# Experts in program order, one hint ahead of each branch, and token gathers by pairs of experts

## The chip, the cores and the metric

The kernel runs on one core of a Trainium2 chip. The metric is the time of one execution on the device in microseconds (us). It is written with a scheduler: the program text lists instructions in an order, the scheduler puts them into the order in which each engine's queue gets them, and it adds the semaphores. Only inside a block under `tc.manual_schedule()` do the engines get them in the order of the text.

## The reference

Two transformer blocks on 256 tokens of 1024 features, all in float32. The first (two layers) and the mixing half of the second are not touched here. The second block ends in a mixture of experts, which is what this case is about. A router gives each token its 4 best of 32 experts and their gates:

```
logits = xt @ w_router + b_router
top_val, top_idx = top_k(logits, 4);  gates = softmax(top_val)
```

For the tokens of an expert `e` it computes

```
gu = x_b @ w_gu[e] + b_gu[e]                      # 1024 -> 2048, gate and up interleaved
gate, up = min(gu[::2], 7), clip(gu[1::2], -7, 7)
((up + 1) * (gate * sigmoid(1.702 * gate))) @ w_dn[e] + b_dn[e]
```

and adds the result, times the gate, to the rows of its tokens. How many tokens an expert has is only known when the router has run. With these inputs, of the experts 1 to 31, 22 have at most 32 tokens, six (4, 13, 21, 24, 26, 30) have 33 to 64, and three (5, 14, 29) have 65 to 96; the profile shows it by which bodies run.

## The kernel before

**Weights.** An expert's weights are 12 tiles of 128 x 2048 float32 (1 MB): eight for gate and up (`ew.first(e)`), four for down (`ew.second(e)`). They pass through 18 buffers. `ew.load(n)` issues loads on SP up to tile `n`; tile `i` takes the buffer of tile `i - 18`, so SP waits until PE has read that one for the last time. The first 18 expert tiles are loaded before the experts start.

**Groups.** Tokens are worked on in groups of 32 (`GROUP`). A group's tokens are gathered by matmuls of the normed tokens `hf` with a one-hot matrix (`gather`, L1763; 32 matmuls in the trace, copied out by ACT and DVE into `xg`). `gather4` (L1773) does it for the first groups of four experts at once, 128 columns, in each fourth expert. `biased` (two matmuls) starts a group's sum in PSUM, `up` (64 matmuls in the trace, L1792) adds the product with the first eight tiles, `swiglu` makes the activation on DVE and ACT, `turn` transposes it (PE, then a copy on ACT into `hT`), `down` (64 matmuls, L1842) multiplies by the last four tiles, `parts` (ACT, DVE) scales by the gate and splits the result in two, and `scatter` (16 matmuls, L1856) adds it to the tokens' rows. The scatter matrix `sT` and the gates `gs` come from `slots_pick` (one-hots on DVE) and `slots` (PE, DVE, ACT).

**Branches.** Each engine reads the expert's count into a register (`values_load`, L1946) and tests it. After the first group's up comes `tc.If(n > 32)` (L1927), whose body gathers the tokens of groups 1 and 2 (`tokens`, 64 columns), runs up, slots, swiglu and turn for group 1, and in an inner `If(n > 64)` for group 2. After the first group's down comes a second `If` (L1942) with down, parts and scatter of those groups, again with an inner one (L1944). An `If` is one unit: nothing moves into it or out of it. At its end each engine sets its semaphore to what the body would have counted, so a buffer that the body could still read comes free for SP only when PE has passed the `If`. `tc.mark_branch_hint_location` writes, on PE, ACT and DVE, a hint that names where the coming branch will go (`label`), from the register `n`.

**Order.** Outside of the `If`s the scheduler chooses. In the trace the loads of the counts and the hints, which depend on nothing but the counts, stand far ahead of their place in the text, and the scatter of the expert before is woven into up. Expert 0 always has two groups, has no branch, and frees its first tiles one by one. A last `If` (L1955, label `more`) holds experts with over 96 tokens; it is not entered here.

The lines that matter below: L1792 up, L1842 down, L1856 scatter, L1825 and L1827 slots, L1809 turn, L1770 gather, L1339 the loads of weights on SP, L1927/L1930 and L1942/L1944 the branches, L1946 the counts, L2187 where the trace books the hints.

Of the kernel before, what the change touches and what calls it, by code (L numbers as in the profile page):

```python
# [74 lines left out]
def program(ctx: ExitStack, tc: tile.TileContext, a, out, dbg=None, upto=99, only=None):  # L75
# [1675 lines left out]
    def experts(hf, pool, ew, rest):  # L1751
        with ExitStack() as p3:
# [20 lines left out]
            def gather4(q):  # L1773

                oh = [same(t, q) for t in range(2)]
                xg = pool.tile([P, 8, P], F32, name="xg4", tag="xg4", bufs=1)
                c = slice(0 if q else GROUP, P)
                gather(xg[:, :, c], [o[:, c] for o in oh])
                return xg

# [6 lines left out]
            def up(ps, xg, W):  # L1787

                for k in range(8):
                    w = W(k)  # L1790
                    for b in range(4):
                        T.matmul(ps[32 * b:32 * b + 32], xg[:, k], w[:, 512 * b:512 * b + 512],  # L1792
                                 start=False, stop=k == 7, skip_group_check=True, tile_position=(0, 32 * b))

            def swiglu(pl, ps):
                gg = pl.tile([P, 256], F32, name="gg", tag="gg", bufs=2)
                V.tensor_scalar(gg, ps[:, :256], 7.0, None, op0=ALU.min)  # L1797
                tu = pl.tile([P, 2, 256], F32, name="etu", tag="etu", bufs=1)
# [5 lines left out]
                return gg  # L1804
# [61 lines left out]
            h0 = [pool.tile([P, 2, P], F32, name=f"hT{g}") for g in range(3)]  # L1866
            sT = [pool.tile([P, 2, 2, P], F32R, name=f"sT{g}") for g in range(4)]
            gs = [pool.tile([P, 1], F32, name=f"gs{g}") for g in range(4)]
# [3 lines left out]
            ohx = [pool.tile([P, 4, GROUP], F32, name=f"ohx{t}") for t in range(2)]  # L1872

            ps = [biased(eg(), 0) for g in range(2)]
            for k in range(8):
                for g in range(2):
                    for b in range(4):
                        T.matmul(ps[g][32 * b:32 * b + 32], ew.xg[:, k, GROUP * g:GROUP * g + GROUP], ew.first(0)(k)[:, 512 * b:512 * b + 512],
                                 start=False, stop=k == 7, skip_group_check=True, tile_position=(0, 32 * b))
                ew.load(NWE + k + 1)  # L1880
                if k == 3:
                    rest()
            hs = [swiglu(pool, p_) for p_ in ps]
            xg = gather4(0)
            ew.bias_of(1)
            for g in range(2):
# [304 lines left out]
```

## Time and profile before

| | |
|---|---|
| Time, median of 3 runs | 2630.83 us (2627.53 to 2643.96) |
| Profiled execution | 2639.72 us |
| Its span, first to last instruction | 2637.7 us |
| Mean granted clock of TensorE | 0.902 |
| Busy share of PE, PEld, DVE, ACT, POOL | 85, 61, 47, 29, 8% |
| DMA over the span | 244 GB/s, 644.16 MB |

PE is TensorE's matmuls, PEld its weight loads, whose queue (PEldq) also holds PE's register, branch and hint instructions. DVE is VectorE, ACT ScalarE, POOL GpSimd and SP SyncE, which only issues transfers. In rows of the timeline the columns are the start in us, the duration, engine, line, operation, output and inputs with their shapes, the count of merged instructions, and in brackets how long the engine had stood idle before and what released it. A busy PE is not a PE at its peak, and shares over the whole span mix stages with different limits: the two blocks ahead of the experts take until about 1505 us.

### The profile page before, as it was taken

The page shows a single profiled execution, that of the slowest core. Times are in us where ns is not written, and L with a number is a line of the kernel's source. Part 1 is how long each engine was busy: PE and PEld are TensorE (multiplying, and loading weights), DVE is VectorE, ACT ScalarE, POOL GpSimd, SP SyncE. Part 2 cuts the span into 40 slices and gives each one's busy share as a digit, 9 for nine tenths or more (in the row PEclk, how much of TensorE's full clock was granted, in tenths as well). Part 3 has the DMA queues.
Part 4 walks back from the last instruction along what each step waited for, and adds up shares of the span by engine and source line. Part 5 has one row for each costly group of instructions (what it writes and reads, how often), then busy time and mean ns, then how long its engine had stood idle before and what let it go on. Part 6 is the DMA issues. An engine that isn't in the chain of part 4 may idle for free. (4 is left out here: it accounts for less than half of the span.)

```text
span 2637.7 us, 43545 instructions
## 1 busy us (share of the span) xinstructions
PE 2230.7 (85%) x18012; PEld 1612.4 (61%) x18012; DVE 1240.6 (47%) x2385; ACT 753.3 (29%) x1336; POOL 203.2 (8%) x188
## 2 busy tenths in 40 slices
PE   8999789999997899988799975876778767787686
PEld 7898678988996679977667532433334324343343
DVE  4667977976657865579865411111111111111111
ACT  3554454444443544465333100000001000000001
POOL 0002310000003300025300000000000000000000
PEclk9999899999999999999889986888778877888897
DMA  8655234444485265442303778689997999888963
GB/s 314 216 194 195 108 133 155 163 145 160 152 322 181 97 266 193 156 135 82 110 17 128 290 318 364 258 328 413 416 378 295 377 417 417 361 339 356 416 284 114
DMA packets 97055, 644.16 MB, mean 244 GB/s; under 512 B 11776, under 2 KB 13312, under 8 KB 23296
## 3 DMA queue, kind: packets, MB, share of 16 engines
q1 hardware_dynamic: 91152, 628.33, 61.0%
q10 hardware_dynamic: 5616, 11.75, 1.4%
q8 instruction: 211, 3.46, 0.5%
q14 instruction: 76, 0.62, 0.1%
HBM read 638.98 MB, written 1.05 MB: 243 GB/s over the span
## 5 line engine op out<-in xcount | busy, mean ns | idle before, releaser
L684 DVE TENSOR_TENSOR wl<-wst,wh 128x1024 fp32r<-128x1024 f32 x298 | 363.7, 1224 | 229.2 <-ACT wh L682 222.6
L749 PE MATMUL gu<-xh,wl 128*128 128x256 f32 x1632 | 459.7, 282 | 7.9 <-DVE wl L684 5.2
L747 PE MATMUL gu<-xh,wh 128*128 128x256 f32 x1632 | 461.5, 283 | 2.1 <-ACT xh L730 1.4
L748 PE MATMUL gu<-xl,wh 128*128 128x256 f32 x1632 | 459.6, 282 | 0.0
L682 ACT CAST wh<-wst 128x1024 fp32r<-128x1024 f32 x320 | 333.5, 1050 | 349.6 <-PE gu L748 203.7
L747 PEld LDWEIGHTS gu<-xh,wh 128*128 128x128 f32 x1632 | 312.8, 192 | 13.4 <-ACT xh L730 3.7
L749 PEld LDWEIGHTS gu<-xh,wl 128*128 128x128 f32 x1632 | 312.7, 192 | 12.3 <-DVE wl L684 6.6
L748 PEld LDWEIGHTS gu<-xl,wh 128*128 128x128 f32 x1632 | 312.7, 192 | 3.2 <-issue 0.3
L1797 DVE TENSOR_SCALAR gg<-eg 128x256 f32<-128x256 f32 x45 | 19.1, 424 | 544.1 <-PE eg L1792 533.1
L1792 PE MATMUL eg<-ew,xg 128*32 128x512 f32 x1984 | 262.4, 672 | 0.0
L1842 PE MATMUL eg<-ew,hT 128*32 128x256 f32 x2880 | 201.9, 446 | 16.9 <-ACT hT L1810 15.5
L1800 ACT ACTIVATE etu<-gg 128x256 f32<-128x256 f32 x45 | 18.7, 416 | 631.3 <-DVE gg L1797 629.2
L1842 PEld LDWEIGHTS eg<-ew,hT 128*32 128x32 f32 x2880 | 101.4, 128 | 111.0 <-issue 40.5
L1792 PEld LDWEIGHTS eg<-ew,xg 128*32 128x32 f32 x1984 | 62.4, 122 | 159.6 <-issue 133.6
L1856 PE MATMUL ac<-y,sT 64*128 64x256 f32 x512 | 54.4, 304 | 102.0 <-PEq L1942 96.9
L104 PE MATMUL acc<-wh,hl 128*128 128x512 f32 x352 | 138.9, 395 | 0.6 <-DVE hl L731 0.6
L103 PE MATMUL acc<-wl,hh 128*128 128x512 f32 x352 | 138.2, 393 | 0.0
L102 PE MATMUL acc<-wh,hh 128*128 128x512 f32 x352 | 138.1, 393 | 0.0
L1856 PEld LDWEIGHTS ac<-y,sT 64*128 64x128 f32 x512 | 39.5, 187 | 146.0 <-issue 144.6
L1433 PE MATMUL pj<-hxH,wl 128*128 128x256 f32 x296 | 88.4, 299 | 14.6 <-DVE wl L1154 13.2
L1825 PE MATMUL ms<-ident,ohs 128*128 128x128 f32 x64 | 17.6, 370 | 98.1 <-PEq L1927 91.3
L1792 PE MATMUL eg<-ew,xgx 128*32 128x512 f32 x768 | 99.0, 674 | 0.0
(560 smaller groups left out, 3586.4 us busy)
## 6 DMA issues: line engine op xcount, KB each, us to landing
ew<-in_wexp SPq DMA_DIRECT2D x384, 1024.0 KB, 15.6
wst<-in_wgu SPq DMA_DIRECT2D x88, 1024.0 KB, 4.8
wst<-in_wd SPq DMA_DIRECT2D x44, 1024.0 KB, 4.8
wada<-in_wada SPq DMA_DIRECT2D x24, 1024.0 KB, 8.7
wst<-in_win SPq DMA_DIRECT2D x20, 1024.0 KB, 4.8
ws<-in_win SPq DMA_DIRECT2D x36, 512.0 KB, 3.8
wst<-in_wout SPq DMA_DIRECT2D x8, 1024.0 KB, 4.8
ws<-in_wup SPq DMA_DIRECT2D x8, 512.0 KB, 4.7
```

The lines of the kernel that those rows point to most:

```text
L102: T.matmul(o, lh, rh, start=start, stop=False)
L103: T.matmul(o, lh, rl, start=False, stop=False)
L104: T.matmul(o, ll, rh, start=False, stop=stop)
L682: S.copy(hi, s_)
L684: (G if kind == SHARED and h else V).tensor_tensor(lo, s_, hi.bitcast(F32), op=ALU.subtract)
L747: T.matmul(o, h[:, c0:c0 + P], st.xh[:, ts, k], start=k == 0, stop=False)
L748: T.matmul(o, h[:, c0:c0 + P], st.xl[:, ts, k], start=False, stop=False)
L749: T.matmul(o, l[:, c0:c0 + P], st.xh[:, ts, k], start=False, stop=k == 7)
L1433: T.matmul(ps[:, j], l[:, c0:c0 + P], hh[:, kk], start=False, stop=kk == 7, skip_group_check=True)
L1792: T.matmul(ps[32 * b:32 * b + 32], xg[:, k], w[:, 512 * b:512 * b + 512], start=False, stop=k == 7, skip_group_check=True, tile_position=( ...
L1842: T.matmul(ps[32 * c:32 * c + 32], hT[:, k % 2, 32 * (k // 2):32 * (k // 2) + 32], w[:, 256 * c:256 * c + 256], start=k == 0, stop=k == 7, ...
L1856: T.matmul(acc[t][h][:, 256 * v:256 * v + 256], sT[hs, v, t], x[hs], start=False, stop=False, skip_group_check=True)
```

## The change

All experts, 0 to 31, are now issued under `tc.manual_schedule()`, on all engines, in the order of the text: one load of the count and one hint ahead of each branch, scatter of the expert before behind the first `If`. Tokens are gathered for a pair of experts, two groups (64 columns) each, in every odd expert, so the second group needs no gather of its own. In the first `If` the second group has only up and swiglu; its slots and turn move into the second `If` (`rest_of`). A third group is gathered alone (32 columns). `gg`, `hT`, `sT` and `gs` have one buffer for the first group and one for further groups (three for `gg`).

```diff
             def same(t, q):
-                o = pool.tile([P, 4, GROUP], F32, name="oh4", tag="oh4", bufs=2)
-                V.tensor_tensor(o, bc(iota[:, :GROUP], 4, 1), bc(pos[t][:, 4 * q:4 * q + 4], GROUP, 2), op=ALU.is_equal)
+                o = pool.tile([P, 2, 2 * GROUP], F32, name=f"oh2{t}", tag=f"oh2{t}", bufs=1)
+                V.tensor_tensor(o, bc(iota, 2, 1), bc(pos[t][:, 2 * q:2 * q + 2], 2 * GROUP, 2), op=ALU.is_equal)
...
-            def gather4(q):
...
-            def up(ps, xg, W):
+            def up_row(ps, x, w, k):
+                for b in range(4):
+                    T.matmul(ps[32 * b:32 * b + 32], x, w[:, 512 * b:512 * b + 512],
+                             start=False, stop=k == 7, skip_group_check=True, tile_position=(0, 32 * b))
+
+            def up(e, xg, W):
+                ps = biased(eg(), e)
                 for k in range(8):
...
+                    up_row(ps, xg[:, k], W(k), k)
+                return ps
...
+            with tc.manual_schedule():
+                ps = [biased(eg(), 0) for g in range(2)]
+                for k in range(8):
                     for g in range(2):
+                        up_row(ps[g], ew.xg[:, k, GROUP * g:GROUP * g + GROUP], ew.first(0)(k), k)
+                    ew.load(NWE + k + 1)
+                    if k == 3:
+                        rest()
+                oh2 = [same(t, 0)[:, 2 * GROUP:] for t in range(2)]
                 for g in range(2):
+                    swiglu(gg[g], ps[g])
+                gather(xg[:, :, 2 * GROUP:], oh2)
+                ew.bias_of(1)
+                slots_pick(oh, 0, 0)
+                slots_pick(ohx, 0, 1)
+                turn(hT, gg[0])
+                turn(hTx, gg[1])
+                slots(sT, gs, oh, 0)
+                parts(y, down(hT, ew.second(0)), gs)
+                slots(sTx, gsx, ohx, 0)
+                parts(yx, down(hTx, ew.second(0)), gsx)
+                ew.load(12 + NWE)
+                slots_pick(oh, 1, 0)
+                scatter(sTx, yx)
...
             def tokens(e, g):
                 for t in range(2):
-                    V.tensor_scalar(ohg[t], iota, float(GROUP * g), pos[t][:, e:e + 1], op0=ALU.add, op1=ALU.is_equal)
+                    V.tensor_scalar(ohg[t], iota[:, :GROUP], float(GROUP * g), pos[t][:, e:e + 1], op0=ALU.add, op1=ALU.is_equal)
                 gather(xgx, ohg)
-            def group_up(e, g, i, W):
-                ps = biased(eg(), e)
-                up(ps, xgx[:, :, GROUP * i:GROUP * i + GROUP], W)
+            def rest_of(e, g, i, W):
                 slots_pick(ohx, e, g)
-                slots(sT[2 + i], gs[2 + i], ohx, e)
-                turn(h0[1 + i], swiglu(mpool, ps))
-            def group_down(i, W):
-                parts(yx, down(h0[1 + i], W), gs[2 + i])
-                scatter(sT[2 + i], yx)
...
+                turn(hTx, gg[i])
+                slots(sTx, gsx, ohx, e)
+                parts(yx, down(hTx, W), gsx)
+                scatter(sTx, yx)
...
+            with tc.manual_schedule():
+                n = count(1)
+                for e in range(1, NE):
+                    W1, W2 = ew.first(e), ew.second(e)
+                    x0 = 2 * GROUP * (e % 2)
+                    if e % 2 and e + 1 < NE:
+                        oh2 = [same(t, (e + 1) // 2) for t in range(2)]
+                    p_ = up(e, xg[:, :, x0:x0 + GROUP], W1)
+                    swiglu(gg[0], p_)
+                    with tc.If(n > GROUP, label=f"u{e}"):
+                        p_ = up(e, xg[:, :, x0 + GROUP:x0 + 2 * GROUP], W1)
+                        swiglu(gg[1], p_)
+                        with tc.If(n > 2 * GROUP):
+                            tokens(e, 2)
+                            swiglu(gg[2], up(e, xgx, W1))
+                    tc.mark_branch_hint_location(f"d{e}", hint=(n > GROUP), engines=engines)
+                    ew.load(12 * e + 8 + NWE)
+                    scatter(sT, y)
+                    slots(sT, gs, oh, e)
+                    if e % 2 and e + 1 < NE:
+                        gather(xg, oh2)
+                    turn(hT, gg[0])
+                    if e + 1 < NE:
+                        ew.bias_of(e + 1)
+                        slots_pick(oh, e + 1, 0)
+                    parts(y, down(hT, W2), gs)
+                    with tc.If(n > GROUP, label=f"d{e}"):
+                        rest_of(e, 1, 1, W2)
+                        with tc.If(n > 2 * GROUP):
+                            rest_of(e, 2, 2, W2)
+                    n = count(e + 1)
+                    if e + 1 < NE:
+                        tc.mark_branch_hint_location(f"u{e + 1}", hint=(n > GROUP), engines=engines)
+                    else:
+                        tc.mark_branch_hint_location("more", hint=(n > GROUPS * GROUP), engines=engines)
+                    ew.load(12 * e + 12 + NWE)
+                scatter(sT, y)
```

`count(e)` is the load of the count, as before (`values_load`).

## Rows read from the trace of the kernel before

**Rows 1.** Windows by stage: us, PE, PEld, DVE, ACT, POOL, PEclk, DMA share, GB/s.

```profile
1505.00:1512.00 7.00, 7.00 (x28) 2.01 (x31) 4.86 (x14) 0.00 (x0) 0.00 (x0) 0.55 0.01 2
...
1512.00:1650.00 138.00, 94.81 (x851) 45.37 (x847) 18.58 (x60) 9.43 (x22) 0.00 (x0) 0.80 0.84 340
...
1650.00:1760.00 110.00, 94.20 (x889) 47.32 (x885) 20.13 (x64) 10.14 (x25) 0.00 (x0) 0.88 0.67 268
...
1760.00:1970.00 210.00, 147.29 (x1181) 70.38 (x1185) 27.17 (x83) 12.69 (x30) 0.00 (x0) 0.80 1.01 416
...
1970.00:2070.00 100.00, 85.55 (x843) 43.86 (x839) 18.60 (x59) 10.28 (x24) 0.00 (x0) 0.90 0.72 287
...
2240.00:2520.00 280.00, 215.06 (x1862) 106.05 (x1861) 41.31 (x128) 20.78 (x49) 0.00 (x0) 0.83 0.91 371
...
2520.00:2610.00 90.00, 78.70 (x795) 36.91 (x798) 14.49 (x45) 8.43 (x20) 0.00 (x0) 0.91 0.54 214
```

**Rows 2.** DMA issues of the page: the expert weights.

```profile
ew<-in_wexp SPq DMA_DIRECT2D x384, 1024.0 KB, 15.6
```

**Rows 3.** Source view, register and branch instructions: count, ns min/median/max, first to last start.

```profile
L1946 PEldq TENSOR_LOAD <-cnt x31: 294/300/321, 1533.4 to 1596.5; - x31
...
L2187 PEldq BRANCH_PREFETCH_HINT  x62: 28/30/44, 1531.6 to 1597.0; - x62
...
L1927 PEldq COMPARE_BRANCH  x31: 73/5942/6882, 1555.0 to 2608.6; - x31
...
L1942 PEldq COMPARE_BRANCH  x31: 77/6112/6407, 1565.9 to 2619.6; - x31
...
L1944 PEldq COMPARE_BRANCH  x18: 76/216/1254, 1685.6 to 2601.3; - x18
```

**Rows 4.** Waits of PE and SP over the experts: us in total, times, longest.

```profile
PE ac L1856 <- PEq L1942: 96.9, 20, 5.1
...
PE ms L1825 <- PEq L1927: 91.3, 20, 17.6
...
SPq L1339 <- PEq L1927: 226.8, 21, 21.9
```

**Rows 5.** Timeline of PE, expert 10: one group.

```profile
1859.26 0.35 PE L1856 MATMUL ac<-y,sT 64*128 64x256 f32 x1 [4.89 <-PEq L1942]
...
1873.88 0.66 PE L1825 MATMUL ms<-ident,ohs 128*128 128x128 f32 x2 [3.76 <-PEq L1927]
...
1876.23 5.49 PE L1842 MATMUL eg<-ew,hT 128*32 128x256 f32 x64 [0.52 <-ACT hT L1810]
...
1886.72 0.47 PE L1856 MATMUL ac<-y,sT 64*128 64x256 f32 x1 [5.00 <-PEq L1942]
```

**Rows 6.** Timeline of PE, parts of experts 5, 7 and 30.

```profile
1716.94 0.44 PE L1809 MATMUL ms<-ident,gg 128*128 128x128 f32 x2 [1.70 <-DVE gg L1803]
...
1717.78 7.08 PE L1792 MATMUL eg<-ew,xgx 128*32 128x512 f32 x64
...
1740.16 3.66 PE L1842 MATMUL eg<-ew,hT 128*32 128x256 f32 x64
...
1744.47 1.49 PE L1856 MATMUL ac<-yx,sT 64*128 64x256 f32 x16 [0.64 <-ACT yx L1847]
...
1785.98 6.32 PE L1770 MATMUL ms<-oh,hf 128*128 128x128 f32 x32
...
2571.01 5.41 PE L1770 MATMUL ms<-ohg,hf 128*128 128x64 f32 x32 [1.71 <-DVE ohg L1905]
```

**Rows 7.** Timeline of PE, experts 29 to 31.

```profile
2500.91 0.35 PE L1856 MATMUL ac<-y,sT 64*128 64x256 f32 x1 [4.91 <-PEq L1942]
...
2559.64 0.28 PE L1856 MATMUL ac<-y,sT 64*128 64x256 f32 x1
...
2601.93 0.38 PE L1856 MATMUL ac<-y,sT 64*128 64x256 f32 x1 [0.82 <-PEq L1944]
...
2615.31 6.28 PE L1842 MATMUL eg<-ew,hT 128*32 128x256 f32 x64 [0.52 <-ACT hT L1810]
```

More of the change, by code (lines that the diff above doesn't have):

```diff
@@ L1872, in experts @@
             ohx = [pool.tile([P, 4, GROUP], F32, name=f"ohx{t}") for t in range(2)]
-            ps = [biased(eg(), 0) for g in range(2)]
-            for k in range(8):
-                for g in range(2):
[L1877 to L1886, printed above, removed]
-                slots_pick((oh, ohx)[g], 0, g)
-                slots(sT[3 * g], gs[3 * g], (oh, ohx)[g], 0)
-            for g in range(2):
-                turn(h0[g], hs[g])
-            for g in range(2):
-                parts((y, yx)[g], down(h0[g], ew.second(0)), gs[3 * g])
-            ew.load(12 + NWE)
+            xg = pool.tile([P, 8, P], F32, name="xg2")
+            with tc.manual_schedule():
+                ps = [biased(eg(), 0) for g in range(2)]
+                for k in range(8):
+                    for g in range(2):
+                        up_row(ps[g], ew.xg[:, k, GROUP * g:GROUP * g + GROUP], ew.first(0)(k), k)
[3 more added lines that the diff above has]
+                oh2 = [same(t, 0)[:, 2 * GROUP:] for t in range(2)]
+                for g in range(2):
+                    swiglu(gg[g], ps[g])
[12 more added lines that the diff above has]
+                scatter(sTx, yx)
             px.close()
@@ L1911, in group_up @@
                 slots_pick(ohx, e, g)
-                slots(sT[2 + i], gs[2 + i], ohx, e)
-                turn(h0[1 + i], swiglu(mpool, ps))
-            def group_down(i, W):
-                parts(yx, down(h0[1 + i], W), gs[2 + i])
-                scatter(sT[2 + i], yx)
-            scatter(sT[3], yx)
-            n = nc.values_load(ew.cnt[0:1, 1:2], min_val=0, max_val=256)
-            for e in range(1, NE):
-                W1, W2 = ew.first(e), ew.second(e)
-                p_ = biased(eg(), e)
-                slots_pick(oh, e, 0)
-                up(p_, xg[:, :, GROUP * (e % 4):GROUP * (e % 4) + GROUP], W1)
-                h = swiglu(pool, p_)
-                with tc.If(n > GROUP, label=f"u{e}"):
-                    tokens(e, 1)
-                    group_up(e, 1, 0, W1)
-                    with tc.If(n > 2 * GROUP):
-                        group_up(e, 2, 1, W1)
-                tc.mark_branch_hint_location(f"d{e}", hint=(n > GROUP), engines=engines)
-                ew.load(12 * e + 8 + NWE)
-                scatter(sT[(e - 1) % 2], y)
-                slots(sT[e % 2], gs[e % 2], oh, e)
-                if e % 4 == 3 and e + 1 < NE:
-                    xg = gather4((e + 1) // 4)
-                turn(h0[0], h)
-                if e + 1 < NE:
-                    ew.bias_of(e + 1)
-                parts(y, down(h0[0], W2), gs[e % 2])
-                with tc.If(n > GROUP, label=f"d{e}"):
-                    group_down(0, W2)
-                    with tc.If(n > 2 * GROUP):
-                        group_down(1, W2)
-                n = nc.values_load(ew.cnt[0:1, e + 1:e + 2], min_val=0, max_val=256)
-                if e + 1 < NE:
-                    tc.mark_branch_hint_location(f"u{e + 1}", hint=(n > GROUP), engines=engines)
-                else:
-                    tc.mark_branch_hint_location("more", hint=(n > GROUPS * GROUP), engines=engines)
-                ew.load(12 * e + 12 + NWE)
```

37 lines of the change are left out of this document (14 added, 23 removed).

## The prediction

> **What bounds the kernel now.** I read the page first (where the time lies), then the windows by stage, the source view of the branches and hints, PE's waits, and last the timeline of single experts. The experts run from about 1505 us to 2622 us of a span of 2637.7 us, so the change can only move these 1117 us.
>
> The DMA engines move 384 weight tiles of 1 MB [rows 2]. In a saturated stretch they run at 1.01 of their time and 416 GB/s (from 1760 us on, [rows 1]), so a tile of 1.049 MB takes 2.52 us and an expert of 12 tiles 30.2 us. Eighteen tiles are there before expert 0 starts; the queue stands at 2 GB/s until 1512 us [rows 1]. The other 366 tiles need 922 us. Against 416 GB/s the other windows lose 138 x (1 - 340/416) = 25 us, 110 x (1 - 268/416) = 39 us, 31 us, 30 us and, at the end, 44 us: 169 us of standing DMA. 1512 + 922 + 169 = 2603, which is where the last weights land. So the stage is limited by DMA except where buffers come free late, and PE frees them.
>
> What PE does in an expert with one group: 27.5 us from 1859.26 to 1886.72 [rows 5]. In it PE stands twice, 3.76 us at the branch of L1927 and 5.00 us at that of L1942. Over the stage this is 91 us and 97 us [rows 4], and SP waits 227 us for PE's sequencer at the first of them before it may issue loads [rows 4]. The cause is in the source view [rows 3]: the branch itself takes 5.9 and 6.1 us on PE (median of 31 each, minimum 0.07, when the body is entered). All 62 prefetch hints of PE stand between 1531.6 and 1597.0 us, while the branches run from 1555 to 2619: the hints and the loads of the counts were moved to the front in a bunch, far from their branches. There they also block PE's queue: one wait at the branch of L1927 is 17.6 us long [rows 4].
>
> **The change, part by part.**
>
> *Hints and loads in program order.* Each count load (0.30 us) and hint (0.03 us) [rows 3] now stands one branch ahead. Between hint and branch PE has 66 matmuls (8 us) or at least 88 (7 us): longer than the 6.1 us of a missed branch. What a hinted jump costs no row shows. Bounds: 0.2 us (median of the short jumps of L1944, which land in code already fetched) and the 6.1 us of today [rows 3]; nothing excludes a half-late hint. I take 0.6 us, near the short jumps, because the lead exceeds the whole miss. That removes some 3.2 us and 4.4 us from each one-group expert. [...] The count load and the join cost PE about 1.2 us per expert, which today is in the bunch.
>
> *Cost of an expert after, on PE at full pace:* load and join 1.2, bias 1.0 (it lies between a turn at 1716.94 and up at 1717.78, so about 0.8, and a little more behind a join), up 7.1, branch 0.6, scatter 1.5, slots to down 2.35 (1873.88 to 1876.23 [rows 5]), down 3.7, branch 0.6 [rows 5, 6]: 18.0 us. Scatter now stands after the first branch and covers the activation chain, where today it is woven into up.
>
> *Pairs.* A gather of 128 columns, 32 matmuls, took 6.32 us [rows 6], in a window whose mean granted clock is 0.80; I take 4.2, an estimate of 0.13 us each at full pace where up's take 7.08/64 = 0.11, and 6.3 as the other end. There are 15 instead of 7, one in each odd expert, but the second group's own gather (5.4 us and 1.71 us of waiting [rows 6], nine times) goes. Mean of a one-group expert: 20.1 us, 10 us under the 30.2 us of DMA. That is the cover for every small wait that program order adds: turn's copy now queues on ACT behind the scaling of sT, gg, hT and sT have one buffer instead of several, and POOL's and SP's branches follow the order; SP's issue order does not change. If PE lost 10 us more per expert, all of it would show.
>
> *Two groups:* second up 8.0 directly behind the first, small branch 0.6, then in the second body turn, slots and the wait for one-hots 3.1 (2.35 and a wait for parts of 0.64), down 3.66, 0.64, scatter 1.49, branch 0.6: 18 + 17.5 = 35 us; expert 30 now takes 42 (2559.64 to 2601.93 [rows 7]); there are six such experts. The first half's buffers come free sooner still, since gather, slots and turn no longer stand ahead of the release. *Three groups:* no gain: the third gather now waits for the second group's activation (1.70 [rows 6]) and its one-hots (1.71), I take 2.8 together, then 5 for the gather and 8 for up: 16.5, and 8.0 for its second half: 59 us, as today (expert 29, 2500.91 to 2559.64 [rows 7]; three such experts).
>
> *The sum.* After, PE is abreast of DMA whenever it meets one-group experts, so a lone two-group expert (35 against 30 us, with ten tiles or 25 us of buffers ahead) makes no DMA wait: 30 us of idle go to 0. At the start 25 go to 15 (the bunch goes; the second half of expert 0, two groups, frees its tiles about 1541, an estimate from its start at 1505 with two ups of 7 to 9, a gather of 4 and two chains of turn, slots and down of 7, while tiles 18 to 25 land by 1532; a further 4 to 5 are lost at expert 1). In the two places where three groups follow two, the fourth-last tile of the triple comes free about 85 us after DMA and PE were abreast, when the 30 tiles that may be out take 76: 12 us, and 5 us more at the next expert, 17 instead of 39 and 31. Idle up to tile 347: 15 + 17 + 17 = 49. Expert 29 starts at 1512 + 330 x 2.52 + 49 = 2393 us; today 2500.9 [rows 7]. From there PE sets the end: expert 29, three groups, is paced by tiles in its first up (20), then 8 + 16.5 + 3.9 + 4.2 (gather) + 3.7 + 17.5 = 74 us; expert 30, two groups, 35; expert 31, 17.5 to the end of down: 2519.5. Today from the end of that down (2615.31 + 6.28 = 2621.6 [rows 7]) to the end of the span are 16.1 us, and the last branch, whose hint stands right before it, keeps its price. Span 2536 instead of 2637.7: **-102 us**. The profiled execution took 2639.7 us, 9 us more than the median of 2630.8; taken off the median: 2529 us.
>
> [...]
>
> **Rivals.** *(B) The hints do nothing,* the branches keep 3.8 and 5.0 us of standing. For it: no row shows a hint closely ahead of its branch, so none shows that one works. Against it: L1944's short jumps are cheap because their code is there, and a hint asks for just that. Then one-group experts are 1.5 us dearer (load, ACT order) x 22 = 33, eight more gathers of 6.3 = 50; two-group experts 7 us cheaper x 6 = 42, the bunch of 17.6 and a smaller one of some 5 gone: +18 us, of which DMA hides about half. 2640 us: no change.
>
> *(C) The hinted block drives out the next one,* so the jump is paid as today and a second fetch follows when PE runs on past the block it landed in. Place: the 44 jumps over bodies; price: one more 4.3 us (mean of 91 + 97 us over 44) each, 189 us on top of B: 2829 us, slower. It decides from the point where a jump costs PE 5.6 us, 1.3 more than now, for there 18.0 - 1.2 + 2.1 + 2 x 5.6 reaches the 30.2 us of DMA and PE is behind everywhere. Against it: bodies that are entered run on through hundreds of instructions today with branches of 0.08 us [rows 3], so code that goes straight on is fetched in time. [...]
>
> **How the numbers follow.** A 0.83, B 0.12, C 0.05. Predicted: A's 2529 us. A's low end: branches at 0.2, gathers waiting 1 us less and half of the idle gone (24), 12 us less in the last three experts: 2493. Its high end: half-late hints at 2.5 us per jump, the lower granted clock in down and gather, which do not hide in the last three experts and around the triples: +35, 2565; with 4 us per jump almost B: 2597. The range is 2493 to 2597. One per cent (26 us) is about what a measurement of this kernel can tell from no change. Faster: A and the low tail of B, 0.85; same: B, 0.09; slower: C and a little for order waits above the cover, 0.06.
>
> **What would show it.** Right: hints spread from 1545 us on, each 7 to 10 us before its branch; PE's branch at a median under 1 us; PE's waits named after L1927 and L1942 in all under 40 us instead of 188, and waits for in_wexp in their place; DMA at 416 GB/s from 2070 to where expert 29 begins near 2393; two-group experts near 35 us. Wrong: branches still at 6 us (B); fetches of code that double while branches stay (C); PE idle behind ACT or DVE by more than 10 us in a one-group expert; or DMA standing in one-group stretches.

## The result and the profile after

The changed kernel takes **2537.85 us** (median of 4 runs, 2533.70 to 2545.72), beside it the kernel before 2631.88 us. The ratio is **0.9633, 95% interval 0.9600 to 0.9665**: 3.7% faster. The prediction was 2529 us, and its range held the time. The profiled execution has a span of 2531.9 us, 105.8 us less than before, at a mean granted clock of 0.93.

The windows by stage, in the columns of [rows 1]; the last two are cut where expert 29 now begins:

```profile
1505.00:1512.00 7.00, 7.00 (x56) 1.82 (x52) 0.24 (x1) 0.00 (x0) 0.00 (x0) 0.76 0.48 163
1512.00:1650.00 138.00, 108.54 (x1103) 54.20 (x1097) 27.82 (x90) 13.39 (x31) 0.00 (x0) 0.93 0.93 379
1650.00:1760.00 110.00, 95.48 (x930) 48.65 (x930) 19.66 (x60) 9.93 (x23) 0.00 (x0) 0.91 0.87 352
1760.00:1970.00 210.00, 154.47 (x1314) 67.25 (x1310) 31.50 (x95) 14.59 (x34) 0.00 (x0) 0.84 0.99 405
1970.00:2070.00 100.00, 78.21 (x852) 39.90 (x848) 19.36 (x60) 10.45 (x24) 0.00 (x0) 0.97 0.97 393
2240.00:2392.00 152.00, 118.93 (x1202) 56.88 (x1206) 27.39 (x84) 13.19 (x31) 0.00 (x0) 0.91 1.01 417
2392.00:2520.00 128.00, 103.52 (x1016) 49.50 (x1008) 21.33 (x63) 11.35 (x27) 0.00 (x0) 0.91 0.68 276
```

The DMA rows rose where they had been low: 340 to 379, 268 to 352, 287 to 393 GB/s [rows 1]. Read as before, the DMA engines now stand 12 + 17 + 6 + 6 = 41 us of the time from 1512 to 2070 us, instead of 25 + 39 + 0 + 31 = 95. That gives back 54 us, and the transfer also starts 4 us sooner (163 GB/s ahead of 1512). From 2240 us to where expert 29 begins the queue no longer stands either (371 GB/s before, 417 now). In the traces the 348th tile, the last one that expert 28 needs, lands at 2391.5 us instead of 2476.4, 85 us sooner.

The source view of hints and branches (count, ns min/median/max, first to last start), for [rows 3]; the branches are now L1929 and L1946:

```profile
L2191 PEldq BRANCH_PREFETCH_HINT  x62: 28/35/44, 1550.8 to 2517.7; - x62
...
L1929 PEldq COMPARE_BRANCH  x31: 76/378/5994, 1545.4 to 2504.2; - x31
...
L1946 PEldq COMPARE_BRANCH  x31: 76/2098/6062, 1561.0 to 2515.5; - x31
```

The hints are spread over the experts: 5.2 to 18.7 us ahead of a skipped first branch (median 6.9), 5.6 to 13.2 us ahead of a skipped second one (median 9.1). The first branch has a median of 0.38 us, but the second still one of 2.1, and both still reach 6. Of the 44 branches that skip a body, 13 take under 0.5 us and 31 over 1 us, 128 us in all (249 before).

The traces also hold the blocks of code, 16 KB each, that the larger of the page's two instruction queues (q8) brings. In all 14 traces together 502 skipped branches take over 1 us, and every one of them ends 1.3 to 1.6 us after such a block has landed; in none of the 101 that take under 0.5 us does a block land. So these branches, called late below, wait for their code. In the kernel before, 37 of 43 late branches get a block that sets out more than 3.3 us after the branch began (median 3.6); in the changed kernel 29 of 31 get one that set out earlier (median 1.8). Of its 30 late branches that have a hint, 28 wait for the second block that sets out behind the hint: the first follows the hint by 0.3 to 3.3 us, the second by 7.2 to 14.8. Which block the hint asked for, the trace does not tell.

The waits of PE and SP, for [rows 4]:

```profile
PE eg L1782 <- DMA ew<-in_wexp: 44.7, 42, 2.6
PE eg L1775 <- PEq L1946: 43.7, 11, 5.3
PE ac L1851 <- PEq L1929: 30.4, 22, 3.7
...
SPq L1339 <- DMA ew<-in_wexp: 520.1, 257, 3.6
...
SPq L1339 <- PEq L1929: 64.6, 10, 10.6
```

PE stands 74 us at the branches instead of 188, and 45 us for weights instead. SP's wait for PE's sequencer at the first branch fell from 226.8 us [rows 4] to 64.6, and its wait for earlier transfers rose from 196.7 us to 520.1: mostly the buffers are now free before the queue wants them.

The timeline of PE where experts 29, 30 and 31 begin, and expert 31's down, for [rows 7]:

```profile
2396.93 0.77 PE L1775 MATMUL eg<-bgh,ob 128*128 128x512 f32 x1 [4.36 <-PEq L1946]
...
2463.36 0.47 PE L1775 MATMUL eg<-bgh,ob 128*128 128x512 f32 x1
...
2497.59 0.47 PE L1775 MATMUL eg<-bgh,ob 128*128 128x512 f32 x1 [2.90 <-issue]
...
2511.57 5.35 PE L1837 MATMUL eg<-ew,hT 128*32 128x256 f32 x64 [1.13 <-ACT hT L1805]
```

Expert 29 starts 104 us sooner than before, so nearly all of the 105.8 us is gained ahead of it: 85 us by its weights, and 19 us because PE, which before began it 24.5 us after the 348th tile had landed, now begins it 5.5 us after. From there on PE sets the end: 66.4 us, 34.2 us and 19.3 us to the end of that down (2516.9), then 15.0 us.

### The profile page after: what moved, and what is told of

It reads as the page before. It is cut to its first block, busy times and chain, and to the rows that moved or that the text cites. A ratio compares the mean times of both kernels' runs of the same rounds, so it can differ in the third digit from the quotient of the medians.

```text
span 2531.9 us, 43693 instructions
## 1 busy us (share of the span) xinstructions
PE 2172.1 (86%) x18076; PEld 1576.2 (62%) x18076; DVE 1248.4 (49%) x2391; ACT 754.8 (30%) x1338; POOL 203.7 (8%) x188
## 3 DMA queue, kind: packets, MB, share of 16 engines
q1 hardware_dynamic: 91152, 628.33, 63.4%
## 5 line engine op out<-in xcount | busy, mean ns | idle before, releaser
L1782 PE MATMUL eg<-ew,xg 128*32 128x512 f32 x2688 | 353.1, 666 | 45.2 <-DMA ew<-in_wexp 44.7
L1782 PEld LDWEIGHTS eg<-ew,xg 128*32 128x32 f32 x2688 | 83.6, 118 | 292.2 <-issue 184.5
L1837 PE MATMUL eg<-ew,hT 128*32 128x256 f32 x2880 | 181.3, 406 | 27.8 <-ACT hT L1805 25.0
L1837 PEld LDWEIGHTS eg<-ew,hT 128*32 128x32 f32 x2880 | 93.8, 117 | 101.8 <-ACT hT L1805 32.8
L1431 PE MATMUL pj<-hxH,wh 128*128 128x256 f32 x296 | 89.7, 303 | 1.7 <-ACT hxH L1412 1.0
L1775 PE MATMUL eg<-bgh,ob 128*128 128x512 f32 x45 | 25.8, 572 | 75.1 <-PEq L1946 43.7
L1432 PE MATMUL pj<-hxL,wh 128*128 128x256 f32 x296 | 88.4, 299 | 0.7 <-DVE hxL L1413 0.7
```

Of the source, the lines that this page charges most:

```text
L1431: T.matmul(ps[:, j], h[:, c0:c0 + P], hh[:, kk], start=kk == j == 0, stop=False, skip_group_check=True)
L1782: T.matmul(ps[32 * b:32 * b + 32], x, w[:, 512 * b:512 * b + 512], start=False, stop=k == 7, skip_group_check=True, tile_position=(0, 32 * b))
L1837: T.matmul(ps[32 * c:32 * c + 32], hT[:, k % 2, 32 * (k // 2):32 * (k // 2) + 32], w[:, 256 * c:256 * c + 256], start=k == 0, stop=k == 7, ...
```

## The experiments

The prediction's reason was: hints in front of their branches make the jumps cheap, and that lets PE keep up with DMA. That is theory A below. Theory B is its main rival: the experts with several groups got shorter, and the hints matter little. All ratios are to the kernel before, with 95% intervals. The lengths that the text uses are these, from the start of one expert's first branch on PE to that of the next (us):

| kernel | ratio | 21 one-group experts, sum | two groups, mean of 6 | three groups, mean of 3 | 44 skipped branches, sum |
|---|---|---|---|---|---|
| before | 1 | 626.8 | 42.3 | 57.7 | 248.7 |
| changed | 0.9633 | 582.5 | 34.6 | 56.3 | 128.1 |
| e1 changed, no hints | 0.9651 | 581.6 | 34.9 | 56.3 | 173.0 |
| e2 before, program order | 0.9981 | 563.1 | 47.3 | 63.6 | 119.4 |
| e3 changed, scheduler's order | 0.9784 | 603.1 | 35.3 | 57.9 | 188.1 |
| e4 half tiles | | 476.5 | 34.6 | 57.5 | 125.8 |
| e5 no pairs | 0.9854 | 565.7 | 44.3 | 63.9 | 135.7 |
| e6 no late turn | 0.9791 | 574.6 | 38.2 | 63.4 | 120.8 |
| e7 half tiles, no hints | | 515.0 | 34.5 | 56.3 | 165.2 |
| e8 two waits away | 0.9577 | 590.2 | 32.2 | 50.5 | 118.7 |
| e9 before, no hints | 0.9844 | 576.2 | 42.7 | 58.8 | 181.2 |
| e10 as e3, no hints | 0.9738 | 596.9 | 35.4 | 58.4 | 172.9 |
| e11 hints in pairs | 0.9550 | 581.2 | 33.3 | 50.2 | 144.8 |
| e12 as e2, no hints | 0.9970 | 573.4 | 47.2 | 60.8 | 206.2 |

**e1: the changed kernel without hints.**

```diff
-                    tc.mark_branch_hint_location(f"d{e}", hint=(n > GROUP), engines=engines)
...
-                    if e + 1 < NE:
-                        tc.mark_branch_hint_location(f"u{e + 1}", hint=(n > GROUP), engines=engines)
-                    else:
-                        tc.mark_branch_hint_location("more", hint=(n > GROUPS * GROUP), engines=engines)
```

> The changed kernel with every branch hint left out; order, pair gathers and late turns stay. 44 branches of the experts jump over their body; in the changed kernel's trace these branches took 129 us of TensorE's time (13 of them about 0.4 us, 31 from 2 to 6 us), in the kernel before 5.9 to 6.1 us each, 264 us in all. Theory A (the hints, now each ahead of its own branch, carry most of the gain): the 135 us that they spared come back, less what the weight DMA covers, and the time goes to 2590 to 2650 us, the skipped branches to about 6 us each. Theory B (the gain is in the order and the shorter many-group experts; late hints are worth little): 2540 to 2560 us, since TensorE then waits for weights less by what it loses at branches.

Measured: 2540.95 us, ratio 0.9651 (0.9608 to 0.9694), not to be told from the time with hints. Theory A falls, and theory B's range holds. The branches did become dearer, as the source view shows:

```profile
L1929 PEldq COMPARE_BRANCH  x31: 70/1289/6316, 1552.5 to 2512.1; - x31
...
L1945 PEldq COMPARE_BRANCH  x31: 73/3907/6277, 1566.0 to 2521.5; - x31
```

and PE's waits show where the 45 us went:

```profile
PE eg L1775 <- PEq L1945: 81.9, 19, 5.5
PE ac L1851 <- PEq L1929: 30.0, 20, 3.9
PE eg L1782 <- DMA ew<-in_wexp: 10.9, 9, 1.6
```

PE stands 38 us more at the second branch and 34 us less for weights. The time that a hint spares there is time in which PE then waits for the next tile. The skipped branch without a hint costs 3.9 us in the mean, not the 5.7 us of the kernel before.

**e2 and e3: the order alone, and the text alone.** e2 emits the text of before, expert 0 included, under program order, so its hints stand in place; e3 is the changed text in the scheduler's order, which bunches the hints and the loads of the counts again (1519 to 1616 us on PE).

```diff
 # e2, against the kernel before
+            with tc.manual_schedule():
                 n = nc.values_load(...)
                 for e in range(1, NE):
...
 # e3, against the changed kernel
-            with tc.manual_schedule():
-                n = count(1)
-                for e in range(1, NE):
+            n = count(1)
+            for e in range(1, NE):
```

> The kernel before with one thing changed: its expert loop, hints included, is emitted in program order on all engines. The gather of four experts' first groups, its way of taking further groups, and the slot one-hots stay as they were. Theory A (order and hints carry the gain; the pair gathers and the late turns only rearrange TensorE's work): 2530 to 2565 us, with the skipped branches at 2 to 3 us in the mean as in the changed kernel. Theory B (the shorter many-group experts carry it): 2595 to 2632 us, experts with two groups as long as before, 42 us. In between, the parts share it.

> The changed kernel's text without program order: the scheduler places the instructions of each engine, as in the kernel before, so it may move the hints away from their branches again. Theory A: the hints bunch ahead of the first branch (62 of them held TensorE for 17.6 us in the kernel before), the skipped branches cost about 6 us again, and the time is 2590 to 2650 us. Theory B: 2540 to 2565 us, since pairs and late turns are still there.

Measured: e2 2631.78 us, ratio 0.9981 (0.9961 to 1.0002): no gain, at the upper end of theory B's range, though its skipped branches take 119 us, less than in the changed kernel. e3 2572.53 us, ratio 0.9784 (0.9734 to 0.9835), between the two theories. So branches at half their price gain nothing with the old text in program order: its two-group experts grow from 42.3 to 47.3 us, where theory B expected no change. PE's waits, before and then in e2, say why in part:

```profile
PE ms L1770 <- DVE ohg L1905: 15.4, 9, 1.7
...
PE ms L1809 <- DVE gg L1803: 12.2, 7, 1.8
...
PE ms L1809 <- DVEq L1930: 8.5, 5, 1.7
```

```profile
PE ms L1809 <- DVE gg L1803: 22.1, 7, 3.2
...
PE ms L1770 <- DVE ohg L1906: 19.3, 9, 2.1
PE ms L1809 <- DVEq L1932: 15.9, 5, 3.2
```

In program order PE stands longer at each turn, until DVE has finished the activation, and at the gather, until DVE has built the one-hots: 57 us in all instead of 36. Expert 30 by windows (columns as in [rows 1]), before, in e2 and in the changed kernel:

```profile
2566.20:2608.60 42.40, 36.44 (x344) 18.17 (x346) 6.80 (x21) 3.74 (x9) 0.00 (x0) 0.88 0.45 173
```

```profile
2544.20:2593.00 48.80, 40.12 (x348) 21.22 (x344) 7.28 (x23) 3.74 (x9) 0.00 (x0) 0.79 0.37 148
```

```profile
2468.30:2504.20 35.90, 29.20 (x312) 12.61 (x308) 6.63 (x20) 3.28 (x8) 0.00 (x0) 0.95 0.50 201
```

From before to e2 the idle time grows by 2.7 us (6.0 to 8.7) and the busy time by 3.7, at a granted clock of 0.79 instead of 0.88; busy time by clock is 32.1 and 31.7, so it is the same work. In expert 30, then, the lower clock is more of the growth than the waits are; over the six experts of two groups, 3.0 of the 5.0 us are idle time and 1.9 are busy time at a mean granted clock of 0.80 instead of 0.87. The changed kernel has 32 matmuls less (the second group's own gather) and 7.2 us less busy time than before; by the same product some 4.9 us of that are less work and 2.3 are the clock. In the traces' records (before and after) the granted clock stands at 0.5 or at 1.0 of full speed; the numbers here are means over a stretch.

**e4 and e7: PE's own pace, with and without hints.**

```diff
-                nc.sync.dma_start(self.W[i], a["wexp"][i // 12, i % 12] if i >= 0 else ...)
+                if i < NWE:
+                    nc.sync.dma_start(self.W[i], a["wexp"][i // 12, i % 12] if i >= 0 else ...)
+                else:
+                    nc.sync.dma_start(self.W[i][:, :1024], a["wexp"][i // 12, i % 12, :, :1024])
...
```

The matmuls of up and down then read the loaded half twice.

> The changed kernel, but from the 19th weight tile on only the first half of each tile is loaded and the matmuls read that half twice, so the weights' transfers are half as long (15 us an expert by the 30.2 us of a whole one) and TensorE's work is the same; the result is not the reference's. It shows TensorE's own pace in the experts and what a hint is worth when one branch follows the other sooner. Theory A (a hint fetches its code in the background however close the branches are): the skipped branches take under 1 us each, a one-group expert some 18 to 20 us, and the time is 2270 to 2340 us. Rival C (code is fetched one block after another, so a hint given less than some 12 us ahead of its branch is late): nearly all of the 44 skipped branches take 2 to 6 us, a one-group expert 24 to 28 us, and the time is 2380 to 2450 us.

> The kernel with half weight tiles (2429.0 us, TensorE sets the pace in nearly every expert), without the branch hints; the result is not the reference's. It shows what the hints spare where TensorE sets the pace. Theory H (the hints help a TensorE-bound stretch, and are only hidden by the weights' transfer in the whole kernel): the skipped branches go from 127 us to 170 us or more and the time rises by as much, to 2465 to 2490 us. Theory N (where TensorE sets the pace the hints are late, and a late hint spares nothing): 2425 to 2445 us.

Measured, one run each: 2429.03 us with hints and 2462.15 us without. The branches in the source view, e4 and then e7:

```profile
L1932 PEldq COMPARE_BRANCH  x31: 76/1980/6116, 1542.9 to 2399.3; - x31
...
L1949 PEldq COMPARE_BRANCH  x31: 76/2195/6275, 1555.8 to 2410.0; - x31
```

```profile
L1932 PEldq COMPARE_BRANCH  x31: 70/1751/4791, 1541.4 to 2432.0; - x31
...
L1948 PEldq COMPARE_BRANCH  x31: 73/4028/8020, 1554.3 to 2441.2; - x31
```

With weights out of the way a one-group expert takes 22.7 us (476.5/21), so PE has 7.5 us to spare under the 30.2 us of a whole expert's transfer; 35 of the 44 skipped branches take over 1 us, against 31 in the changed kernel. So rival C of e4's expectation holds in its time (2380 to 2450 us) and broadly in its branches (31 of 44 over 2 us): a hint was late more often here, where the branches follow closer. The one-group expert, 22.7 us, lies between theory A's 18 to 20 and rival C's 24 to 28. Theory H of e7 holds in kind: leaving the hints out costs 39 us of branches and 33 us of time, with the time 3 us under its range and the branches (165 us) 5 us under. This is the gain that the whole kernel hides. It rests on one run of each kernel; the 33 us are nearly three times the spread of the runs of the changed kernel (12 us, lowest to highest).

**e5 and e6: pairs against late turning.** e5 takes the pair gathers out, e6 puts slots and turn of further groups back into the first body.

```diff
 # e5
-                        p_ = up(e, xg[:, :, x0 + GROUP:x0 + 2 * GROUP], W1)
+                        tokens(e, 1)
+                        p_ = up(e, xgx, W1)
...
-                    if e % 2 and e + 1 < NE:
+                    if e % 4 == 3 and e + 1 < NE:
                         gather(xg, oh2)
...
 # e6
                         swiglu(gg[1], p_)
+                        turned(e, 1, 1)      # slots_pick, slots, turn
...
                             swiglu(gg[2], up(e, xgx, W1))
+                            turned(e, 2, 2)
```

> The changed kernel without the pair gathers: four experts' first groups are gathered at once, and a second group's tokens are gathered inside the body that uses them, as in the kernel before; program order, hints and the late turning of further groups stay. With the order alone the time did not move (2631.8 us) and six experts of two groups were 47 us long, against 34.6 us in the changed kernel. Theory P (most of the gain of a two-group expert is that its tokens are there when its body begins): two-group experts 41 to 46 us, time 2580 to 2620 us. Theory L (most of it is the late turning, which spares TensorE the waits for VectorE's swiglu inside the body): 35 to 39 us, 2545 to 2570 us.

> The changed kernel with the pair gathers, but the slots and the turning of further groups stand in the first body, right behind their swiglu, as in the kernel before. Theory P: two-group experts 36 to 39 us, time 2545 to 2570 us. Theory L: 41 to 46 us, 2580 to 2620 us. If both parts count alike, this run and the one before it lie between, near 2570 to 2585 us each.

Measured: e5 2597.85 us, ratio 0.9854 (0.9817 to 0.9892); e6 2574.69 us, ratio 0.9791 (0.9750 to 0.9832). With e2 and the changed kernel they make a square (not an exact one, for e2 also gathers groups 1 and 2 together and has other buffers): late turning is worth 34 us without pairs (2632 to 2598) and 37 us with them (2575 to 2538), pairs 57 us (2632 to 2575) and 60 us (2598 to 2538). Within the error the two parts add up. Theory P is right that pairs count more, in e5 to the letter (44.3 us); in e6 it was 5 us too low, and there the late turn is worth 7 us in each three-group expert besides 3.6 us in each of two. Lines of expert 30 that belong to the two parts (busy us, mean ns, idle before), in e5 and in e6:

```profile
L1770 PE MATMUL ms<-ohg,hf 128*128 128x32 f32 x32 | 6.3, 372 | 2.2 <-DVE ohg L1906 2.2
```

```profile
L1820 PE MATMUL ms<-ident,ohx 128*128 128x128 f32 x2 | 0.5, 328 | 2.2 <-DVE ohx L1812 2.2
```

e5 pays 8.5 us for the second group's gather and the wait ahead of it. The wait in e6 is 1.0 us in the changed kernel, and expert 30 takes 35.9 us in both, so the waits do not carry the late turn's worth alone. Means over the six experts of two groups (us, and PE's granted clock):

| kernel | length | PE busy | PE idle | clock | busy x clock |
|---|---|---|---|---|---|
| before | 42.3 | 36.5 | 5.9 | 0.87 | 31.8 |
| e2 before, program order | 47.3 | 38.4 | 8.9 | 0.80 | 30.7 |
| e5 no pairs | 44.3 | 36.8 | 7.5 | 0.85 | 31.3 |
| e6 no late turn | 38.2 | 32.2 | 5.9 | 0.86 | 27.7 |
| changed | 34.6 | 29.6 | 5.0 | 0.95 | 28.0 |

Pairs take away work (the gather). Between e6 and the changed kernel the work is the same, 0.9 of the 3.6 us are idle time, and the rest is the clock. Why the granted clock is higher in the changed kernel no run here takes apart.

**e9, e10 and e12: hints and order, taken apart.** Each is an earlier kernel (before, e3, e2) less its hint lines. In the scheduler's order (e9, e10) the loads of the counts then leave the front too: on PE they stand from 1570 to 2569 us in e9, and from 1545 to 2544 in e10. So these two runs take away the bunch of hints and loads together.

> The kernel before without its branch hints, nothing else changed. Its 62 hints stand in a bunch before 1597 us, on TensorE too, and every skipped branch still took about 6 us. Theory Q (the bunch itself cost time at the start of the experts; 17.6 us were waited there once): the experts start their weights' transfer sooner and the time falls to 2612 to 2625 us. Rival (the bunch hides beside loads of instructions that are needed anyway, or the scheduler fills the place with another wait): 2627 to 2640 us.

> The changed kernel's text in the scheduler's order and without hints, so that only the order differs from the changed kernel without hints (2541 us). With the hints the scheduler's order took 2572.5 us, 35 us more than program order. Theory Q (what program order is worth is that it keeps the hints out of one bunch): 2540 to 2552 us. Rival S (the scheduler's order of the other instructions costs the time, TensorE's slots and scatters ahead of a wait): 2562 to 2580 us.

> The kernel before in program order (2631.8 us with its hints in place) and without hints; it is the last of eight combinations of text (old, new), order (scheduler's, program's) and hints (with, without). Theory D (hints in place spare little, and program order lengthens the old text's many-group experts because TensorE stands at its own waits there): two-group experts stay near 47 us, and the time is 2625 to 2645 us, so that program order costs the old text some 40 us and gains the new one 24. Rival (it is the hints that spoil the old text in any order): two-group experts near 42 us, 2585 to 2605 us.

Measured: e9 2591.11 us, ratio 0.9844 (0.9786 to 0.9901); e10 2564.88 us, 0.9738 (0.9686 to 0.9791); e12 2629.19 us, 0.9970 (0.9948 to 0.9991). e9 was the surprise: taking the hint lines out of the kernel before gains 1.6%, 45 us (2636.66 us beside it), where theory Q expected 12 to 25. Its branches:

```profile
L1927 PEldq COMPARE_BRANCH  x31: 70/2792/6317, 1547.8 to 2556.7; - x31
...
L1941 PEldq COMPARE_BRANCH  x31: 73/4067/6062, 1555.7 to 2566.4; - x31
```

With the bunch the medians were 5.9 and 6.1 us [rows 3], without it 2.8 and 4.1. Experts 1 to 3 together take 77.5 us instead of 97.5; there the bunch stands on PE's queue, and most of it is the loads (31 x 0.30 us against 62 x 0.03 us of hints, [rows 3]). The other 18 one-group experts become another 31 us shorter (626.8 - 576.2 - 20). So the bunch not only stood in the way, the branches stayed dearer long after it: in e9 only 7 of 42 late branches get a block of code that sets out more than 3.3 us after the branch, against 37 of 43 before.

In the new text this does not come again. From e3 to e10 experts 1 to 3 also become 21 us shorter (96.5 to 75.4), but the 44 branches go only from 188 to 173 us, 15 of 40 and 18 of 35 of the late ones get their block late, and the ratios, 0.9784 and 0.9738, are within the error. So what e9 gains late in the experts need not come from the hints as such: a rival that no run takes out is that without the hint lines every later instruction stands at another place in its block of code. In e10 rival S holds in its time: 2564.9 us in the scheduler's order against 2541.0 in program order; which instruction's place costs it was not taken apart. In e12 theory D holds; its waits of PE are those of e2, with the branches on top:

```profile
PE eg L1783 <- PEq L1943: 67.0, 19, 5.5
PE ac L1856 <- PEq L1929: 65.6, 22, 5.3
...
PE ms L1809 <- DVE gg L1803: 22.1, 7, 3.2
PE ms L1770 <- DVE ohg L1906: 19.3, 9, 2.1
```

Eight combinations are then measured (ratios):

| | old text | new text |
|---|---|---|
| scheduler's order, hints in a bunch | 1 | 0.9784 |
| scheduler's order, no hints | 0.9844 | 0.9738 |
| program order, no hints | 0.9970 | 0.9651 |
| program order, hints in place | 0.9981 | 0.9633 |

Along one path, the 3.7% are: bunch gone 1.6, new text 1.1, program order 0.9, hints in place 0.2 (inside the error). Along another path the parts have other sizes. With the bunch still there the new text gains 2.2%, and the bunch then costs 0.5 (inside the error). Program order costs the old text 1.3% and gains the new one 0.9%; the waits of PE on DVE that it lengthens in the old text are in part gone from the new one (the second group's gather and its one-hots), which fits the sign, though no run takes it apart. What all paths share is that hints in place are worth nothing clear of the error in either text, as long as the weight tiles are whole.

**e8: two waits of PE on DVE taken away.**

```diff
 # one-hots for the second and third group ahead of the second group's swiglu
+                        tokens(e, 2)         # one-hots only
+                        slots_pick(ohx, e, 1)
                         swiglu(gg[1], p_)
                         with tc.If(n > 2 * GROUP):
-                            tokens(e, 2)
+                            gather(xgx, ohg)
...
 # up: the bias matmuls behind seven rows
-                ps = biased(eg(), e)
-                for k in range(8):
-                    up_row(ps, xg[:, k], W(k), k)
+                ps = eg()
+                for k in range(7):
+                    up_row(ps, xg[:, k], W(k), k, k == 0)
+                T.matmul(ps, o, bgh, ...); T.matmul(ps, o, bgl, ...)
+                up_row(ps, xg[:, 7], W(7), 7)
```

> The changed kernel with two waits of TensorE on VectorE taken away: the one-hots for the second and third group are built ahead of the second group's swiglu (TensorE waited 8.9 us in 9 places and 6.7 us in 3 for them), and the bias matmuls of an expert's first product stand behind seven of its eight rows (they waited 16.8 us in 8 places for VectorE's branch and 8.8 us for its one-hots). Theory B (the experts of several groups set the end): of these 41 us the part in the last three experts and in the stretches in which the weights' transfer stands comes off, 8 to 20 us: 2518 to 2530 us. Rival (what TensorE does not wait for there it waits for next, the weights or the next branch): 2533 to 2543 us.

Measured: 2519.97 us, ratio 0.9577 (0.9546 to 0.9608), 18 us less than the changed kernel: theory B. The experts with three groups fall from 56.3 to 50.5 us, those with two from 34.6 to 32.2. PE's waits:

```profile
PE eg L1782 <- DMA ew<-in_wexp: 60.0, 61, 2.7
PE eg L1782 <- PEq L1952: 41.3, 10, 5.6
PE ac L1855 <- PEq L1933: 18.2, 19, 5.5
PE eg L1782 <- DVEq L1952: 16.2, 8, 6.4
```

The waits for the one-hots of further groups (8.9 and 6.7 us) are gone, and that for the pair's one-hots fell from 8.8 to 2.7 us. The wait behind DVE's branch (16.8 us in the changed kernel, now 16.2) stayed; it only moved from the bias to the first row of up. The two edits were not run apart.

**e11: both hints of an expert together,** on top of e8.

```diff
-                    tc.mark_branch_hint_location(f"d{e}", ...)
+                    if e == 1:
+                        tc.mark_branch_hint_location(f"d{e}", ...)
...
                         tc.mark_branch_hint_location(f"u{e + 1}", ...)
+                        tc.mark_branch_hint_location(f"d{e + 1}", ...)
```

> The changed kernel with the two waits taken away (2520.0 us), and the hint for an expert's second branch moved directly behind the hint for its first one, so that it is given more than 20 us ahead of its branch instead of 7 to 11. Theory F (code comes one block after another, whatever the hints ask for): the second branch now comes in time (TensorE's idle time there falls from 59 us to under 20), the first one less often (17.9 us now, up to 60), and the time stays within 2512 to 2526 us. Rival G (a hint holds until its branch comes): both are in time, TensorE's idle time at the 44 skipped branches falls from 77 to under 25 us, and the time to 2500 to 2512 us. Rival W (the second hint throws out what the first one fetched): the first branches take 4 to 6 us each, and the time rises to 2526 to 2545 us.

Measured: 2515.73 us, ratio 0.9550 (0.9500 to 0.9601), not to be told from e8. Its branches:

```profile
L1933 PEldq COMPARE_BRANCH  x31: 76/3272/6235, 1550.8 to 2482.3; - x31
...
L1953 PEldq COMPARE_BRANCH  x31: 73/360/6136, 1564.7 to 2493.8; - x31
```

The medians have changed places (e8: 0.38 and 2.1 us): the branch that is hinted far ahead is mostly in time, the other late. Rival G falls. It is theory F in kind, though PE still stands 28 us at the second branch, more than the 20 us that F allowed; the first branch's loss looks like W in single experts (up to 6.2 us), but W's time did not come. e11 and e8 are both faster than the changed kernel.

## Why the prediction was right, and where it was not

The time came out, and so did the picture of DMA and of the experts with several groups. The reason that the text gave the most weight, that hints in place make the jumps cheap, did not: without any hint the changed kernel takes the same time within the error (e1). That the number still came out is luck in part, as the fourth point below says.

**Tile price and standing DMA: right.** 2.52 us a tile at 416 GB/s held (417 GB/s from 2240 to 2392 us). Idle DMA up to the last three experts was put at 15 + 17 + 17 = 49 us; the windows give 12, 17 and 12. Expert 29 was to start at 2393 us and started at 2396.9. In the kernel before the last weights land at 2608.6 us, 6 us after the text's 2603.

**The last three experts: right but for one size.** 74 + 35 + 17.5 + 16.1 were predicted, 66.4 + 34.2 + 19.3 + 15.0 measured. The three-group expert was put 8 us too high, mostly in its first up (20 us, measured 15.6 from 2396.93 to the next bias at 2412.50) and in its last part (17.5 us, measured 14.9). The span was put at 2536 us and is 2531.9.

**Two-group experts by pairs: right.** 35 us predicted, 34.6 measured. It needs pairs and late turning together (e6 without late turning: 38.2) and the higher granted clock that comes with them (0.95, in e6 0.86). That the gather per pair costs nothing to see, because one-group experts have room under DMA, is argued from their 7.5 us of room (e4); no run leaves the gather out there.

**The hinted jump at 0.6 us: wrong.** This is the step that failed. The text reasoned that a lead of 7 to 8 us exceeds the whole miss of 6.1 us. The 44 jumps cost 2.9 us in the mean (128.1/44). The lead did not decide here: the second branch has the longer one (9.1 against 6.9 us, medians) and is the later one. In 28 of 30 late jumps PE waits for the second block of code that sets out behind the hint, 7.2 to 14.8 us after it, and no lead of 7 to 8 us covers that. PE's waits at the two branches were to fall under 40 us and are 74; the second branch's median was to be under 1 us and is 2.1. By the prediction's own scale (2565 us at 2.5 us a jump, 2597 at 4) the time should have been near 2570. That scale failed too: e1 pays 3.9 us a jump and takes 2541 us. The cover that the text gave a one-group expert, 10 us below DMA's 30.2, absorbs such a jump; e4 measures the room at 7.5 us with late hints, e7 at 5.7 us without any (515.0/21 = 24.5), one run each. The two errors cancelled, and the number came out: that is luck.

**Rival B's price: wrong by 100 us.** "The hints do nothing" was put at 2640 us; e1, with no hints at all, takes 2541. B kept the standing of 3.8 and 5.0 us as the price of a jump without help. e9 shows that those were the jumps of a kernel with a bunch of hints and loads in it; without the bunch they are cheaper (medians of 2.8 and 4.1 us instead of 5.9 and 6.1). B also let DMA hide half of what was added, and it hid nearly all. The prediction counted the bunch as one wait of 17.6 us and some idle DMA at the start; taking it out of the old text alone is worth 1.6%.

**Rival C: refuted.** That a hinted block drives out the next one was an assumption of the author's, which no run shows. The page counts 211 blocks in the larger of the two instruction queues before, 208 after and 213 in e1; of these 129, 125 and 131 come from 1505 us on. No second fetch per jump appears, and the jumps got cheaper, not dearer.

**Program order taken as free: right for the new text only.** The text gave it 10 us of cover. In the new text it is free (e1 against e10 even gains 24 us). e2 and e12 show that this was a property of the new text, not of the order.

## What to carry to other kernels

Price a latency where it is paid: here the same late jumps cost 33 us when PE sets the pace and 3 us when the weights do, so look first at which stretch has which limit. Before crediting a hint, a prefetch or an order with a gain, run the kernel without it: here a bunch of hints and loads was worse than none in one text, and the price of "no help" could not be read from a trace that had the bunch in it. The same order cost one text 1.3% and gained another 0.9%, so measure an order on the text that it is for. When a stretch gets shorter, split it into work, idle time and clock before naming the cause.

## What the runs showed of the hardware

- A branch that skips a body took PE under 0.5 us (101 of them) or, where it waited for a block of code, mostly 2 to 6 us; each of the 502 late ones in these traces ends 1.3 to 1.6 us after a 16 KB block has landed. Without hints, in e1, the medians were 1.3 and 3.9 us.
- In the old text, hints and loads of counts bunched far ahead of their branches go with dearer branches for the next 1000 us: 5.9 and 6.1 us on PE against 2.8 and 4.1 without, and at L1927 93 against 45 ns on ACT and 116 against 56 ns on DVE (medians, before and e9). In the new text ACT and DVE show the same at L1927 (93 against 45 and 116 against 56 ns, e3 and e10), but PE's 44 branches cost 188 against 173 us. Why it lasts in the one and not in the other is open.
- With both hints of an expert given together (e11) the second branch's median falls from 2.1 to 0.36 us, and the first one's rises from 0.38 to 3.3.
- The same work of expert 30 (344 and 348 matmuls in the trace) kept PE busy for 36.4 us at a mean granted clock of 0.88 and for 40.1 us at 0.79 (before and e2). Why the clock was lower in e2 is open.
